# Strassen-Winograd feed-forward pairs on one Trainium2 core: the seventh product held in its place, and the first two pairs' weight sets made back to back

## The chip, the cores and the metric

The kernel runs on one core of one Trainium2 chip. The core has a matrix engine (TensorE, PE in the profile), three engines for element work (VectorE, DVE in the profile; ScalarE, ACT; GpSimd, POOL), a queue that only issues transfers (SyncE, SP), and 16 DMA engines that all queues share. PSUM is the memory that the matrix engine writes; SBUF holds everything else. The metric is the device time of one execution in microseconds (us); smaller is better.

## The reference

Two layers, each over 512 tokens of width 1024 in float32:

```python
for i in range(DEPTH):                       # 2 layers
    xn = rmsnorm(x, norm1_g[i])
    u_pool, q, k, v, g_a, g_b = split(xn @ w_in[i])
    o = diff_attention(norm_rope(q), norm_rope(k), v, lam)
    merged = sigmoid(g_a) * pool_mixer(u_pool) + sigmoid(g_b) * rmsnorm(o)
    x = x + merged @ w_out[i]
    hn = rmsnorm(x, norm2_g[i])
    gate, up = split(hn @ w_ffn_in[i])       # 1024 -> 2 x 2816
    x = x + (silu(gate) * up) @ w_ffn_out[i] # 2816 -> 1024
```

The part at hand is `hn @ w_ffn_in`, with `silu(gate) * up` behind it.

## The kernel before

Every float32 operand of the big products is cut into a high part of reduced precision (type fp32r, names ending in h or hi) and the rest (l or lo), and each product is three matmuls: high x high, high x low, low x high. The high part of a weight is a cast on ScalarE (L182), the low part a difference on VectorE (L183); `split` does both.

The feed-forward input product runs per pair of hidden blocks: a `Ffn(f0)` makes 256 gate and 256 up columns for all 512 tokens. Gate and up, and the two halves of the model width and of the tokens, are treated as a 2x2 block product in Winograd's form: seven products of 24 matmuls (128x256 each, lines L263, L265, L266 in `pair_product`) in place of eight. Each product `self.p(n, ...)` has a weight set `self.sets[n]`, a high and a low tile of 128x1024:

- 1 and 2: the weight blocks A11 and A12 themselves, made by `gate`
- 5: S1 = A21 + A22 (L654)
- 6: S2 = S1 - A11 (L656)
- 7: S3 = A11 - A21 (L655)
- 3: S4 = A12 - S2 (L663)
- 4: A22 itself

The other side of each product, sums of token blocks, is made once per layer by `Quarters.put` while the tokens' norm comes in (L360 to L369, tiles xq, xr, xt).

Two ways make a low part. `parts(src)` takes the difference on VectorE. `parts(src, piece_no)`, used for blocks that are weights as they lie in memory (A22 here), casts on ScalarE (L217), writes the negated high part to the low tile on ScalarE (L218), and lets a transfer from GpSimd's queue add the weight from HBM onto it (L219, 512 KB).

The tiles rotate: six high and six low weight tiles (`SPLITS`), seven raw tiles (`RAWS`) for loaded blocks and their sums. A set is begun when an earlier set's product has been read and its tile is free; a load is issued when a raw tile is free.

A pair's products stand in the code in the order 1, 6, 5, 2, 7, 3, 4 (`first`, `rest`, `second`): p6 and p7 go into one PSUM tile (b, an mm tile), p5 and p3 into another (c, an mm tile), p4 into a third (d, a tr tile), p1 and p2 into an sc tile. Between them ScalarE and VectorE copy and add these (L693, L696, L701, L704, L706, L711), and `swiglu` makes the hidden values (L611 to L613, fh and fl by L182 and L183).

The first two pairs of a layer, f0 = 0 and 2, are special: their sets 1 and 2 are made while the attention output is projected, p1 and p2 of both run as the tokens' norms arrive, and then `ffn_start` runs for each of the two `sums()` (the other five sets) and `rest()` (the other five products). The nine later pairs run one at a time in `ffn_in`, with `sums(True)`.

Instructions are not run in the order of the code: a scheduler that has its own costs places them on each engine, and may move an instruction ahead of others that it does not depend on. On the chip each engine then takes them strictly in that placed order.

Of the kernel before, what the change touches and what calls it, by code (L numbers as in the profile page):

```python
# [104 lines left out]
def trunk_kernel(  # L105
# [11 lines left out]
    nc = tc.nc  # L117
# [4 lines left out]
    def mm_ps():  # L122
        return ps.tile([P, 512], F32, name="mm", tag="mm", bufs=3)
# [4 lines left out]
    def tr_ps():  # L128
        return ps.tile([P, 512], F32, name="tr", tag="tr", bufs=2)
# [50 lines left out]
    def split(hi, lo, src):  # L180

        ins = nc.scalar.copy(hi, src)  # L182
        nc.vector.tensor_sub(lo, src, hi.bitcast(F32))  # L183
        return ins
# [17 lines left out]
    def loaded():  # L202

        i = at[0]
        at[0] += 1
        raw = sb.tile([P, 4, VD], F32, name="raw", tag="raw", bufs=RAWS)
        nc.sync.dma_start(raw.rearrange("p a b -> p (a b)"), wts[i])
        return i, raw

    def parts(src, piece_no=None):  # L210

        hi = sb.tile([P, 4, VD], F32R, name="whi", tag="whi", bufs=SPLITS)
        lo = sb.tile([P, 4, VD], F32R, name="wlo", tag="wlo", bufs=SPLITS)
        if piece_no is None:
            split(hi, lo, src)
        else:
            nc.scalar.copy(hi, src)  # L217
            nc.scalar.activation(lo, src, AF.Copy, scale=-1.0)  # L218
            nc.gpsimd.dma_start(lo.rearrange("p a b -> p (a b)"), wts[piece_no], accum_op=ALU.add)  # L219
        return hi, lo  # L220
# [15 lines left out]
    def run_due(done=None):  # L236

        if running[0]:
            return
        running[0] = True  # L240
        while waiting and (waiting[0][0] <= clock[0] if done is None else not done()):
            heapq.heappop(waiting)[2]()
        running[0] = False
        assert done is None or done()
# [11 lines left out]
    def pair_product(acc, a, b, start):  # L256

        for i in range(2):
            for k in range(4):
                run_due()  # L260
                ah, al = (x[:, k, i * P:(i + 1) * P] for x in a)
                bh, bl = (x[:, k, :] for x in b)
                nc.tensor.matmul(acc[:, i, :], lhsT=ah, rhs=bh, start=start and not i and not k, stop=False,  # L263
                                 skip_group_check=True)
                nc.tensor.matmul(acc[:, i, :], lhsT=ah, rhs=bl, start=False, stop=False, skip_group_check=True)  # L265
                nc.tensor.matmul(acc[:, i, :], lhsT=al, rhs=bh, start=False, stop=i == 1 and k == 3, skip_group_check=True)  # L266
                clock[0] += 3 * acc.shape[-1]

    def transpose(dst, src):
        nc.tensor.transpose(dst, src, ident)  # L270
        clock[0] += 2 * P
# [16 lines left out]
    def need(*keys):  # L288
        run_due(lambda: all(k in ready for k in keys))
# [136 lines left out]
    for layer in range(L):  # L426
# [191 lines left out]
        def hidden_pair(f0):  # L618
            tag = HIDDEN_AT[f0]
            if tag in ("u", "m", "mj"):  # L620
                hh, hl = (sb.tile([P, 2, S], F32R, name="f" + part, tag=tag, bufs=2) for part in "hl")
                return [(hh[:, i, :], hl[:, i, :]) for i in range(2)]
            tags = (("pr0", 2), ("pr1", 2)) if tag == "pr" else (("up", 2), ("us", 2))
            out = []
            for tg, bufs in tags:
                out.append([sb.tile([P, S], F32R, name="f" + part, tag=tg, bufs=bufs) for part in "hl"])
            return out

        class Ffn:
# [15 lines left out]
            def sums(self, a12=False):  # L645

                _, r21 = loaded()
                n22, r22 = loaded()
                if a12:
                    self.gate_raw(1)  # L650
                s1 = sb.tile([P, 4, VD], F32, name="ws", tag="raw", bufs=RAWS)
                if a12:
                    self.gate(0, self.n11)
                nc.vector.tensor_add(s1, r21, r22)  # L654
                nc.vector.tensor_sub(r21, self.r11, r21)  # L655
                nc.vector.tensor_sub(self.r11, s1, self.r11)  # L656
                self.sets[6] = parts(self.r11)
                self.sets[5] = parts(s1)
                if a12:
                    self.gate(1, self.n12)  # L660
                else:
                    self.sets[4] = parts(r22, n22)
                nc.vector.tensor_sub(self.r12, self.r12, self.r11)  # L663
                self.sets[7] = parts(r21)
                self.sets[3] = parts(self.r12)
                if a12:
                    self.sets[4] = parts(r22, n22)
                self.to = hidden_pair(self.f0)
                for i in range(2):
                    hidden[self.f0 + i] = self.to[i]  # L670
# [4 lines left out]
            def p(self, n, acc, start=True):  # L675
                q = quarters[-1]
                x = {1: q.b11, 2: q.b21, 3: q.b22, 4: q.t4, 5: q.t1, 6: q.t2, 7: q.t3}[n]
                pair_product(acc, self.sets[n], x, start)

            def first(self):  # L680
                self.a = s_ps().rearrange("p (i c) -> p i c", i=2)
# [7 lines left out]
            def rest(self, second=False):  # L689
                b, c = (mm_ps().rearrange("p (i c) -> p i c", i=2) for _ in range(2))  # L690
                self.p(6, b)
                x2 = self.temp("qn", 3)
                nc.vector.tensor_add(x2, b, self.x1)  # L693
                self.p(5, c)
                p5 = self.temp("ah")
                nc.scalar.copy(p5, c)  # L696
                if second:
                    self.second()
                self.p(7, b, False)
                x3 = self.temp("ta", 2)  # L700
                nc.vector.tensor_add(x3, b, self.x1)  # L701
                self.p(3, c, False)
                c22 = self.temp("pwl")
                nc.vector.tensor_add(c22, x3, p5)  # L704
                c12 = self.temp("al")
                nc.vector.tensor_add(c12, c, x2)  # L706
                swiglu(self.to, 1, c12, c22)
                d = tr_ps().rearrange("p (i c) -> p i c", i=2)
                self.p(4, d)
                c21 = self.temp("pwh")  # L710
                nc.vector.tensor_add(c21, d, x3)  # L711
                swiglu(self.to, 0, self.a, c21)

        quarters, early = [], []
# [48 lines left out]
        def ffn_start():  # L763
            need(*((f"h{layer}", t) for t in range(2)))
            for x in early:
                x.first()
            for x in early:
                x.second()
            need(*((f"h{layer}", t) for t in range(2, 4)))
            for x in early:  # L770
                x.sums()
                x.rest()

        def ffn_out(f0, f1, last):
# [78 lines left out]
```

## Time and profile before

| what | value |
|---|---|
| three runs | 1456.76, 1457.75, 1459.85 us; median 1457.75 |
| profiled execution, its own time | 1456.47 us |
| its span, first to last instruction | 1454.4 us |
| PE busy in the span | 1435.9 us (99%) |
| VectorE busy | 980.6 us (67%) |
| ScalarE busy | 692.8 us (48%) |
| mean granted TensorE clock | 0.998 |
| stretch in which the two special pairs run, layer 1 | about 379 to 432 us |
| the same in layer 2 | about 1099 to 1152 us |

The profiled execution lies 0.3 us under the fastest of the three runs; of its time 2.1 us are outside the span. Times in rows are microseconds from the span's start. In a row `mm<-xqh,wlo` names what is written and what is read. A bracket at a row's end, such as `[2.19 <-DMA wlo<-in_wts]`, is idle time of the engine just before the instruction, and what ended it. Since matmuls are pipelined, a 128x256 matmul is shown as 0.28 us long, while the next one starts 0.12 us after it. In a row of windows a pair such as `47.81 (x379)` is busy time and instructions of one engine, and the fields after POOL are the granted TensorE clock, the mean busy share of the DMA engines and GB/s.

### The profile page before, as it was taken

The page shows a single profiled execution, that of the slowest core. Times are in us where ns is not written, and L with a number is a line of the kernel's source. Part 1 is how long each engine was busy: PE and PEld are TensorE (multiplying, and loading weights), DVE is VectorE, ACT ScalarE, POOL GpSimd, SP SyncE. Part 2 cuts the span into 40 slices and gives each one's busy share as a digit, 9 for nine tenths or more (in the row PEclk, how much of TensorE's full clock was granted, in tenths as well). Part 3 has the DMA queues.
Part 4 walks back from the last instruction along what each step waited for, and adds up shares of the span by engine and source line. Part 5 has one row for each costly group of instructions (what it writes and reads, how often), then busy time and mean ns, then how long its engine had stood idle before and what let it go on. Part 6 is the DMA issues. An engine that isn't in the chain of part 4 may idle for free.

```text
span 1454.4 us, 21625 instructions
## 1 busy us (share of the span) xinstructions
PE 1435.9 (99%) x8390; PEld 1266.9 (87%) x8390; DVE 980.6 (67%) x1820; ACT 692.8 (48%) x1319; POOL 115.3 (8%) x149
## 2 busy tenths in 40 slices
PE   8999999999989999999999999999999999999999
PEld 6888888888889989989888888888888998999897
DVE  6767676666888548737576686665758985487462
ACT  6544353444656346516354443434446663464350
POOL 1010000100001001001010001001000110010000
PEclk9999999999999999999999999999999999999999
DMA  7321231224168457818422132222422683585261
GB/s 280 109 73 58 95 116 59 88 74 115 39 165 208 126 129 176 217 44 211 138 85 81 59 116 74 80 75 72 131 58 73 170 213 115 128 187 174 69 163 58
DMA packets 49208, 170.92 MB, mean 118 GB/s; under 512 B 5585, under 2 KB 6481, under 8 KB 49106
## 3 DMA queue, kind: packets, MB, share of 16 engines
q1 hardware_dynamic: 38882, 134.41, 28.2%
q0 software_dynamic: 8928, 32.51, 12.6%
q10 hardware_dynamic: 1296, 2.62, 0.6%
q8 instruction: 66, 1.08, 0.3%
q14 instruction: 36, 0.29, 0.1%
HBM read 167.42 MB, written 2.10 MB: 117 GB/s over the span
## 4 chain that ended last, share of the span: by engine, by line
PE 92%; issue 3%; DVE 2%; DMA 2%; ACT 1%; POOL 0%; POOLq 0%; DVEq 0%
PE mm L251 19%; PE mm L253 19%; PE mm L252 19%; PE mm L266 5%; PE mm L263 5%; PE mm L265 5%; PE sc L265 3%; PE sc L266 3%; PE sc L263 3%; PE tr L270 3%; DMA wlo<-in_wts 1%; PE tr L266 1%; PE tr L263 1%; PE tr L265 1%; DVE wlo L183 1%
## 5 line engine op out<-in xcount | busy, mean ns | idle before, releaser
L182 ACT CAST whi<-raw 128x1024 fp32r<-128x1024 f32 x226 | 237.4, 1052 | 210.8 <-issue 120.1
L183 DVE TENSOR_TENSOR wlo<-raw,whi 128x1024 fp32r<-128x1024 f32 x226 | 274.6, 1221 | 81.7 <-ACT whi L182 77.5
L251 PE MATMUL mm<-whi,xh 128*128 128x512 f32 x512 | 205.9, 402 | 0.2 <-ACT xh L182 0.2
L252 PE MATMUL mm<-wlo,xh 128*128 128x512 f32 x512 | 200.3, 391 | 0.4 <-DVE wlo L183 0.4
L253 PE MATMUL mm<-whi,xl 128*128 128x512 f32 x512 | 200.6, 392 | 0.0
L602 DVE TENSOR_TENSOR res<-mm,res 128x512 f32<-128x512 f32 (+1 forms) x97 | 66.1, 684 | 118.7 <-PE mm L253 118.6
L253 PE MATMUL mm<-whi,fl 128*128 128x512 f32 (+1 forms) x358 | 138.5, 387 | 0.0
L251 PE MATMUL mm<-whi,fh 128*128 128x512 f32 (+1 forms) x358 | 138.3, 387 | 0.0
L252 PE MATMUL mm<-wlo,fh 128*128 128x512 f32 (+1 forms) x358 | 138.2, 387 | 0.0
L253 PEld LDWEIGHTS mm<-whi,xl 128*128 128x128 f32 x512 | 96.2, 188 | 21.0 <-DVE xl L183 0.2
L280 POOL TENSOR_TENSOR r<-r,mhalf 128x1 f32<-128x1 f32 (+1 forms) x80 | 60.3, 754 | 673.7 <-DVE r L279 553.2
L252 PEld LDWEIGHTS mm<-wlo,xh 128*128 128x128 f32 x512 | 96.7, 189 | 18.3 <-DVE wlo L183 0.9
L251 PEld LDWEIGHTS mm<-whi,xh 128*128 128x128 f32 x512 | 96.5, 188 | 18.4 <-ACT xh L182 0.6
L266 PE MATMUL mm<-xqh,wlo 128*128 128x256 f32 x352 | 101.2, 288 | 4.7 <-DVE wlo L183 4.7
L219 POOL DMA_DIRECT2D wlo<-in_wts x62 | 54.3, 876 | 614.9 <-ACT wlo L218 328.2
L251 PE MATMUL mm<-xh,whi 128*128 128x512 f32 x256 | 102.0, 398 | 0.0
L265 PE MATMUL mm<-xql,whi 128*128 128x256 f32 x352 | 100.9, 287 | 0.0
L263 PE MATMUL mm<-xqh,whi 128*128 128x256 f32 x352 | 100.9, 287 | 0.0
L265 PE MATMUL sc<-xql,whi 128*128 128x256 f32 x352 | 99.9, 284 | 0.8 <-DVE xql L183 0.8
L253 PE MATMUL mm<-xh,wlo 128*128 128x512 f32 x256 | 99.9, 390 | 0.0
L266 PE MATMUL sc<-xqh,wlo 128*128 128x256 f32 x352 | 99.7, 283 | 0.3 <-DMA wlo<-in_wts 0.3
L263 PE MATMUL mm<-xrh,whi 128*128 128x256 f32 x352 | 99.8, 283 | 0.0
(161 smaller groups left out, 3455.0 us busy)
## 6 DMA issues: line engine op xcount, KB each, us to landing
raw<-in_wts SPq DMA_DIRECT2D x244, 512.0 KB, 4.3
wlo<-in_wts POOLq DMA_DIRECT2D x62, 512.0 KB, 7.6
pwr<-in_pool_w ACTq DMA_DIRECT2D x8, 256.0 KB, 2.7
out<-res SPq DMA_DIRECT2D x7, 256.0 KB, 2.0
res<-in_x SPq DMA_DIRECT2D x3, 512.0 KB, 8.2
g<-in_gains SPq DMA_DIRECT2D x6, 256.0 KB, 3.2
res<-in_x ACTq DMA_DIRECT2D x1, 512.0 KB, 3.9
lv<-in_rows SPq DMA_DIRECT2D x2, 256.0 KB, 5.5
```

The costliest lines, as they stand in the source:

```text
L182: ins = nc.scalar.copy(hi, src)
L183: nc.vector.tensor_sub(lo, src, hi.bitcast(F32))
L219: nc.gpsimd.dma_start(lo.rearrange("p a b -> p (a b)"), wts[piece_no], accum_op=ALU.add)
L251: nc.tensor.matmul(acc, lhsT=ah, rhs=bh, start=i == 0, stop=False)
L252: nc.tensor.matmul(acc, lhsT=ah, rhs=bl, start=False, stop=False)
L253: nc.tensor.matmul(acc, lhsT=al, rhs=bh, start=False, stop=i == n - 1)
L263: nc.tensor.matmul(acc[:, i, :], lhsT=ah, rhs=bh, start=start and not i and not k, stop=False, skip_group_check=True)
L265: nc.tensor.matmul(acc[:, i, :], lhsT=ah, rhs=bl, start=False, stop=False, skip_group_check=True)
L266: nc.tensor.matmul(acc[:, i, :], lhsT=al, rhs=bh, start=False, stop=i == 1 and k == 3, skip_group_check=True)
L270: nc.tensor.transpose(dst, src, ident)
L280: nc.gpsimd.tensor_tensor(r, r, mhalf[:, :width], op=ALU.pow)
L602: nc.vector.tensor_add(res[t][:, cs], here, res[t][:, cs])
```

## The change

Three edits. `pair_product` returns its last matmul, and `rest` places all matmuls of p4 behind the last matmul of p3 of the same pair on the matrix engine. In `sums`, for the first two pairs (a12 false), A22's set is made second, right behind set 6, and S3's set (7) comes ahead of S4's difference and set (3); the later pairs keep their order 6, 5, 2, 7, 3, 4. `ffn_start` makes the sets of both pairs before the `rest` of the first.

```diff
@@ pair_product
-                nc.tensor.matmul(acc[:, i, :], lhsT=al, rhs=bh, start=False, stop=i == 1 and k == 3, skip_group_check=True)
+                last = nc.tensor.matmul(acc[:, i, :], lhsT=al, rhs=bh, start=False, stop=i == 1 and k == 3,
+                                        skip_group_check=True)
                 clock[0] += 3 * acc.shape[-1]
+        return last
@@ Ffn.sums
                 self.sets[6] = parts(self.r11)
+                if not a12:
+                    self.sets[4] = parts(r22, n22)
                 self.sets[5] = parts(s1)
                 if a12:
                     self.gate(1, self.n12)
                 else:
-                    self.sets[4] = parts(r22, n22)
+                    self.sets[7] = parts(r21)
                 nc.vector.tensor_sub(self.r12, self.r12, self.r11)
-                self.sets[7] = parts(r21)
+                if a12:
+                    self.sets[7] = parts(r21)
                 self.sets[3] = parts(self.r12)
                 if a12:
                     self.sets[4] = parts(r22, n22)
@@ Ffn.p
-                pair_product(acc, self.sets[n], x, start)
+                return pair_product(acc, self.sets[n], x, start)
@@ Ffn.rest
-                self.p(3, c, False)
+                third = self.p(3, c, False)
...
-                self.p(4, d)
+                with tc.issue_after(third.ins):
+                    self.p(4, d)
@@ ffn_start
             for x in early:
                 x.sums()
+            for x in early:
                 x.rest()
```

No instruction and no transfer is added or taken away. On PE, outside the two special pairs of each layer (and the first matmuls of p1 of the pair behind them), the order is the same as before.

The first place is PE at the end of the first pair's p5 (tile mm_3880 before, mm_3912 in the change; tr_3995 is p4's tile, wlo_3864 the low part of A22's set, whi_3873 and wlo_3874 are set 3). Before:

```order
L265 MATMUL mm_3880<-xql_3470,whi_3859 128x256
L266 MATMUL mm_3880<-xqh_3469,wlo_3860 128x256
L263 MATMUL tr_3995<-xth_3473,whi_3863 128x256
L265 MATMUL tr_3995<-xtl_3474,whi_3863 128x256
L266 MATMUL tr_3995<-xth_3473,wlo_3864 128x256
```

With the change:

```order
L265 MATMUL mm_3912<-xql_3470,whi_3864 128x256
L266 MATMUL mm_3912<-xqh_3469,wlo_3865 128x256
L263 MATMUL mm_3912<-xqh_3469,whi_3873 128x256
L265 MATMUL mm_3912<-xql_3470,whi_3873 128x256
L266 MATMUL mm_3912<-xqh_3469,wlo_3874 128x256
```

Where p4's first matmuls stood right behind p5, p3's now stand: its first 18, then the 24 of p7, the last 6 of p3, and p4's 24.

The second place is VectorE while the last tokens' sums and the first pair's sets are made (wlo_3860 is set 5 before, wlo_3870 set 7, wlo_3874 set 3; L663 is S4, L654 the second pair's sum S1). Before:

```order
L183 TENSOR_TENSOR wlo_3860<-ws_3851,whi_3859 128x1024
L183 TENSOR_TENSOR xrl_3472<-xd_3783,xrh_3471 128x4x128
L366 TENSOR_TENSOR xd_3784<-xd_3792,tr_3772 128x512
L183 TENSOR_TENSOR xql_3470<-xd_3792,xqh_3469 128x4x128
L369 TENSOR_TENSOR xd_3785<-xw_3649,xd_3783 128x512
L183 TENSOR_TENSOR xrl_3472<-xd_3784,xrh_3471 128x4x128
L663 TENSOR_TENSOR raw_3483<-raw_3483,raw_3479 128x1024
L183 TENSOR_TENSOR xtl_3474<-xd_3785,xth_3473 128x4x128
L183 TENSOR_TENSOR wlo_3870<-raw_3847,whi_3869 128x1024
L183 TENSOR_TENSOR wlo_3874<-raw_3483,whi_3873 128x1024
L693 TENSOR_TENSOR cqn_3905<-mm_3879,cqn_3740 128x512
L654 TENSOR_TENSOR ws_4034<-raw_4030,raw_4032 128x1024
```

With the change (wlo_3869 is set 7, L667 is S4, L656 the second pair's S1, wlo_3874 set 3; set 5 stands four rows above the first one shown):

```order
L183 TENSOR_TENSOR wlo_3869<-raw_3847,whi_3868 128x1024
L183 TENSOR_TENSOR xrl_3472<-xd_3783,xrh_3471 128x4x128
L368 TENSOR_TENSOR xd_3784<-xd_3792,tr_3772 128x512
L183 TENSOR_TENSOR xql_3470<-xd_3792,xqh_3469 128x4x128
L371 TENSOR_TENSOR xd_3785<-xw_3649,xd_3783 128x512
L183 TENSOR_TENSOR xrl_3472<-xd_3784,xrh_3471 128x4x128
L667 TENSOR_TENSOR raw_3483<-raw_3483,raw_3479 128x1024
L183 TENSOR_TENSOR xtl_3474<-xd_3785,xth_3473 128x4x128
L656 TENSOR_TENSOR ws_3883<-raw_3879,raw_3881 128x1024
L183 TENSOR_TENSOR wlo_3874<-raw_3483,whi_3873 128x1024
```

Sets 5 and 7 moved up among the tokens' sums, and the second pair's S1 moved from behind set 3 to ahead of it.

The third place is VectorE at the second pair's sets (wlo_4043, wlo_4053, wlo_4057 are its sets 5, 7, 3 before). Before:

```order
L706 TENSOR_TENSOR cal_3985<-mm_3880,cqn_3905 128x512
L183 TENSOR_TENSOR wlo_4039<-raw_3481,whi_4038 128x1024
L711 TENSOR_TENSOR cpwh_4020<-tr_3995,cta_3957 128x512
L612 SCALAR_TENSOR_TENSOR th_3987<-th_3987,cal_3985 128x512
L612 SCALAR_TENSOR_TENSOR th_4022<-th_4022,sc_3685 128x512
L613 SCALAR_TENSOR_TENSOR th_3987<-th_3987,cpwl_3983 128x512
L613 SCALAR_TENSOR_TENSOR th_4022<-th_4022,cpwh_4020 128x512
L183 TENSOR_TENSOR fl_3878<-th_3987,fh_3877 128x256 x2
L183 TENSOR_TENSOR fl_3878<-th_4022,fh_3877 128x256 x2
L183 TENSOR_TENSOR wlo_4043<-ws_4034,whi_4042 128x1024
L183 TENSOR_TENSOR wlo_4053<-raw_4030,whi_4052 128x1024
L183 TENSOR_TENSOR wlo_4057<-raw_3485,whi_4056 128x1024
```

With the change (wlo_3888, wlo_3897, wlo_3901, wlo_3906 are its sets 6, 5, 7, 3):

```order
L183 TENSOR_TENSOR wlo_3888<-raw_3481,whi_3887 128x1024
L706 TENSOR_TENSOR cta_3989<-mm_3911,cqn_3740 128x512
L711 TENSOR_TENSOR cal_4017<-mm_3912,cqn_3937 128x512
L709 TENSOR_TENSOR cpwl_4015<-cta_3989,cah_3963 128x512
L183 TENSOR_TENSOR wlo_3897<-ws_3883,whi_3896 128x1024
L183 TENSOR_TENSOR wlo_3901<-raw_3879,whi_3900 128x1024
L183 TENSOR_TENSOR wlo_3906<-raw_3485,whi_3905 128x1024
L614 SCALAR_TENSOR_TENSOR th_4019<-th_4019,cal_4017 128x512
L717 TENSOR_TENSOR cpwh_4052<-tr_4027,cta_3989 128x512
```

The second pair's sets now stand ahead of the first pair's hidden values, where they stood behind them. On ScalarE the two steps of A22's set, cast and negated copy (L217, L218), likewise moved up: for the first pair the copy stands 12 instructions earlier, and for the second pair ahead of the first pair's hidden values. The order of the loads on SyncE and of the accumulating loads on GpSimd is unchanged.

## The prediction

> **What bounds the kernel now.** I read the page first, then PE's waits, the span in windows, and PE's timeline at the waits.
>
> ```profile
> span 1454.4 us, 21625 instructions
> PE 92%; issue 3%; DVE 2%; DMA 2%; ACT 1%; POOL 0%; POOLq 0%; DVEq 0%
> ```
>
> The chain that ended last is PE for 92%: the kernel goes as fast as PE is fed. So a change that leaves PE's 8390 matmuls alone can win only PE's waits, and these are few:
>
> ```profile
> PE tr L266 <- DMA wlo<-in_wts: 4.7, 2, 2.5
> PE mm L266 <- DVE wlo L183: 4.7, 2, 2.3
> PE sc L265 <- DVE xql L183: 0.8, 2, 0.4
> PE sc L266 <- DMA wlo<-in_wts: 0.3, 1, 0.3
> ...
> 379.00:432.00 53.00, 47.81 (x379) 46.87 (x379) 49.14 (x68) 32.52 (x47) 4.07 (x5) 0.97 0.45 121
> 432.00:1099.00 667.00, 666.81 (x3809) 584.98 (x3808) 440.47 (x840) 313.23 (x612) 52.73 (x66) 1.00 0.41 115
> 1099.00:1152.00 53.00, 47.72 (x381) 46.98 (x380) 48.79 (x68) 32.56 (x47) 4.06 (x5) 0.97 0.45 121
> ```
>
> Above the dots are PE's waits (total us, times, longest), below them windows. PE idles 5.2 us in 379 to 432, 5.3 us in 1099 to 1152, and 0.2 us in the 667 us between: both layers wait where the two special pairs run, and nearly nowhere else. The timeline there:
>
> ```profile
> 393.21 0.28 PE L263 MATMUL mm<-xrh,whi 128*128 128x256 f32 x1
> ...
> 398.85 0.28 PE L266 MATMUL mm<-xqh,wlo 128*128 128x256 f32 x1
> 398.97 0.28 PE L263 MATMUL tr<-xth,whi 128*128 128x256 f32 x1
> 399.09 0.28 PE L265 MATMUL tr<-xtl,whi 128*128 128x256 f32 x1
> 401.55 0.39 PE L266 MATMUL tr<-xth,wlo 128*128 128x256 f32 x1 [2.19 <-DMA wlo<-in_wts]
> ...
> 413.60 0.28 PE L265 MATMUL sc<-xql,whi 128*128 128x256 f32 x1
> 416.22 0.39 PE L266 MATMUL mm<-xqh,wlo 128*128 128x256 f32 x1 [2.34 <-DVE wlo L183]
> ```
>
> The first wait is p4 of the first pair, moved up in front of p3, with A22's low part still on its way; the second is p5 of the second pair, waiting for set 5's difference. PE steps by 0.12 us, so a matmul's tail of 0.16 us counts as busy in each wait and is lost as well. Behind the second wait the clock drops:
>
> ```profile
> 396.77:400.18 3.41, 2.60 (x22) 2.40 (x20) 3.41 (x5) 1.64 (x2) 0.00 (x0) 1.00 0.83 186
> 400.18:403.59 3.41, 2.04 (x17) 2.04 (x18) 3.34 (x4) 0.00 (x0) 0.00 (x0) 1.00 0.98 338
> 413.84:417.25 3.41, 1.07 (x9) 1.03 (x9) 3.41 (x7) 2.51 (x4) 1.44 (x2) 1.00 0.24 54
> 417.25:420.66 3.41, 3.41 (x18) 3.41 (x17) 3.38 (x5) 0.09 (x1) 0.32 (x1) 0.50 1.02 187
> 1137.46:1140.87 3.41, 3.41 (x18) 3.41 (x18) 3.38 (x5) 0.00 (x0) 0.52 (x1) 0.50 0.97 213
> ```
>
> After a stretch with 1.07 us of PE work in 3.41 the granted clock is 0.50 for the next 3.41 us, in both layers; after the first wait, spread over two such stretches (2.60 and 2.04 us of work), it stays 1.00.
>
> **What the change takes away.** First wait: 4.7 + 2 x 0.16 = 5.0 us over both layers. p4 is now behind p3 on PE, so it comes some 8 us later, and its set's copy moves up:
>
> ```profile
> 383.79 1.05 ACT L217 CAST whi<-raw 128x1024 fp32r<-128x1024 f32 x1
> 392.38 1.06 ACT L218 ACTIVATE wlo<-raw 128x1024 fp32r<-128x1024 f32 x1
> 399.17 0.59 ACT L696 COPY cah<-mm 128x512 f32<-128x512 f32 x1 [0.81 <-PE mm L266]
> 393.74 0.90 POOL L219 DMA_DIRECT2D wlo<-in_wts  x1 [9.25 <-DVE xrl L183]
> 415.76 1.81 POOL L219 DMA_DIRECT2D wlo<-in_wts  x2 [21.13 <-ACT wlo L218]
> 436.68 0.86 POOL L219 DMA_DIRECT2D wlo<-in_wts  x1 [6.13 <-ACT wlo L218]
> ...
> DMA to landing us min/median/max: 5.5/9.1/12.5
> ```
>
> L218 takes the place where L217 ran, at 383.8; the accumulating load goes out near 385.1 and, even with the longest landing here (12.5 us, 376 to 450), is in by 397.6, 9 us before p4. Second wait: 4.7 + 0.3 = 5.0 us. The second pair's set 5 now stands ahead of the first pair's hidden values on VectorE; by the rows below it is ready 2 to 3 us ahead of PE. The 0.3 us wait, with its tail 0.4, belongs to a load that went out within a microsecond of another (415.76, x2); now it goes out alone. Half clock: 2 x 3.41 x 0.50 = 3.4 us. Together 5.0 + 5.0 + 0.4 + 3.4 = 13.8 us.
>
> **What takes its place.** The first wait had hidden something: set 3 was late too.
>
> ```profile
> 395.99 1.23 DVE L663 TENSOR_TENSOR raw<-raw 128x1024 f32<-128x1024 f32 x1
> 397.13 0.69 DVE L183 TENSOR_TENSOR xtl<-xd,xth 128x512 fp32r<-128x512 f32 x1
> 397.73 2.36 DVE L183 TENSOR_TENSOR wlo<-raw,whi 128x1024 fp32r<-128x1024 f32 x2
> 400.00 0.69 DVE L693 TENSOR_TENSOR cqn<-mm,cqn 128x512 f32<-128x512 f32 x1
> 400.60 1.22 DVE L654 TENSOR_TENSOR ws<-raw 128x1024 f32<-128x1024 f32 x1
> 401.86 1.22 DVE L655 TENSOR_TENSOR raw<-raw 128x1024 f32<-128x1024 f32 x1
> ```
>
> The x2 row is sets 7 and 3: set 3 is there at 400.09. In the new order the same instructions stand ahead of it, only shuffled, and one more: the second pair's S1 (L654 before), a step of 401.86 - 400.60 = 1.26 us. So set 3 is ready at 401.35. PE starts p6 at 393.21 as before, has 48 matmuls of p6 and p5 (5.76 us) and two of p3, and asks for set 3's low part at 399.21. **New wait A: 2.2 us in each layer**, 4.4 in all. Its lower end is 0.9 us (set 3 no later than before), its upper end is the rival on the load below. From there VectorE has five steps of 1.14 to 1.26 and four of 0.6 to the start of the second pair's set 5 (third place of the change) and 1.2 for itself: 400.1 + 6.0 + 2.4 + 1.2 = 409.7. PE, at p3's third matmul at 401.35, has 94 matmuls of p3, p7, p4 and p6 (11.3 us) and two of p5, and asks at 412.9: the old second wait has 3 us of cover.
>
> p3 adds to the tile that p5 filled, so it needs p5's copy to be done: that copy began 0.32 us after p5's last matmul (398.85 to 399.17) and takes 0.59, some 1.0 us with the way back. In the first pair A covers it. In the second pair three of p3's matmuls are moved ahead of p7, behind only two of the next pair's p1, so 3 steps of 0.12 cover 0.36. **New wait B: 0.6 us a layer**, 1.2 in all; none below, since nothing else stands there, and 1.0 at most.
>
> PE then comes 6.9 - 2.2 - 0.6 = 4.1 us earlier to the next pair, whose own A22 load goes out at 436.68 and is asked for here:
>
> ```profile
> 446.62 0.28 PE L266 MATMUL tr<-xth,wlo 128*128 128x256 f32 x1
> ```
>
> With the median landing it is in at 445.8, 0.8 us ahead. If its chain of casts moves up with PE, which frees its tiles, this costs nothing; if the chain doesn't move at all, 4.1 - 0.8 = 3.3 us a layer. **New wait C: 0.5 us a layer**, nearer to nothing because every set there has a tile to wait for; 1.0 in all.
>
> The rest I cost at nothing. Set 7's cast and difference now stand ahead of the last tokens' xr parts and push these by about 1.1 us; p6's second matmul, which needs the low one, is put 14 matmuls (1.7 us) later on PE and covers it. VectorE is 49.14 of 53.0 us busy in the stretch: if it had to do all of that work within it, at most 3.9 us a layer could be won, 7.7 in all.
>
> Sum: 1456.47 - 13.8 + 4.4 + 1.2 + 1.0 = 1449.3 us on the profiled execution's scale, a gain of 7.2, just inside VectorE's 7.7. The profiled execution is 1.3 us under the median of the three runs (1457.75); half-clock stretches that fall otherwise may be why, and these go. I carry half of it: **1450.0 us**.
>
> **Rivals.** (1) The new wait A trips the half clock in both layers: 2 x 1.7 = 3.4 us more, 1453.4. For it: two waits of 2.3 us did. Against: two others as long did not, and A is shorter, with two matmuls in it. The Trainium skill ("TensorE: Matmul & The Clock Gate", section "HAM oscillation") wants PE gaps to stay under some 3.4 us; by that rule no wait here would throttle, this rival would have no chance, and 1450.0 would stand. The trace disagrees on the length and agrees that the stretch is 3.41 us, and the trace decides. (2) C at its upper end: 2 x 2.8 more, 1455.6. For it: the margin of 0.8 us; against: the chain hangs on tiles that PE frees. (3) Slower: in the new order VectorE stands at the second pair's S1 with set 3 behind it, and S1 needs the second pair's two loads. The second of these goes out when S1 of the first pair has been read for set 5, near 391.4 (set 5 starts right behind the row that began at 389.46).
>
> ```profile
> 389.46 0.69 DVE L360 TENSOR_TENSOR xd<-tr,xw 128x512 f32<-128x512 f32 x1
> ...
> DMA to landing us min/median/max: 3.2/4.8/11.1
> ```
>
> That is the landing of raw tiles (376 to 450). VectorE reaches S1 near 398.9, so the median leaves 2.7 us to spare. Each microsecond past 398.9 is one more of A. From 402.3 on, 10.9 us after issue, A is 5.6 and with the half clock the layer loses 5.6 + 1.7 + 0.6 + 0.5 = 8.4 us instead of 6.9: 1460 us with both layers and the 0.7 carried. Only the longest landing gets there, and I take that for one of the loads beside the two accumulating ones of 415.76. (4) A shrinks to 0.9 and C to nothing: 1446.4. (5) PE's order comes out of the scheduler without effect: 1457.75; the placed order shows p4 behind p3, so hardly.
>
> **How the numbers follow.** Forecast, 1446.5 to 1452.5 on its own: 0.62. Rival 1: 0.13, rival 2: 0.12, rival 3: 0.05, rival 4: 0.06, rival 5: 0.02. The range takes in rival 4 with the carried 0.7 gone, rival 1 and nearly all of rival 2: 1445.5 to 1455.0. A measurement tells 0.2%, or 2.9 us, from no change: faster means under 1454.8. That is the forecast, rival 4, most of rival 1 and under half of rival 2 (C between its ends), 0.84; rival 3 is slower, 0.05; 0.11 stay within.
>
> **What would show it.** PE's waits: "tr L266 <- DMA" and "mm L266 <- DVE" at the second pair's p5 are gone; in their stead one wait of some 2 us for VectorE's wlo at the first pair's third p3 matmul, and one of 0.6 for ScalarE's copy of p5 in the second pair. No window with clock 0.50 near 417 and 1137. VectorE's S1 of the second pair starts without waiting for a load. The 432 to 1099 stretch keeps its 0.2 us of idle time, bar C. It is wrong if p3's wait is over 4 us, if a DMA ends it, if a 0.50 window stands behind it, or if the next pair's p4 waits more than a microsecond.

## The result

| | median us | lowest to highest | runs |
|---|---|---|---|
| before | 1457.26 | 1455.62 to 1459.87 | 6 |
| changed | 1449.88 | 1448.39 to 1452.14 | 6 |

The ratio is 0.9946, 95% interval 0.9934 to 0.9959: 7.4 us or 0.5% faster. The forecast was 1450.0. A second series of the changed kernel, on the chip of the experiments, has a median of 1449.53 (0.9950, 0.9936 to 0.9963). The profiled execution took 1450.88 us.

The page and PE's waits, first of the changed kernel (total us, times, longest):

```profile
span 1449.1 us, 21617 instructions
PE 94%; DVE 4%; ACT 1%; issue 1%; POOL 0%; DMA 0%; POOLq 0%; ACTq 0%; DVEq 0%
...
PE mm L263 <- ACT cah L701: 2.6, 4, 0.8
PE mm L266 <- DVE wlo L183: 1.5, 2, 0.8
```

DMA has gone from the chain, and with it every wait of PE for an accumulating load (4.7 and 0.3 us) and for the second pair's set 5 (4.7). In their place stand waits for ScalarE's copy of p5 (cah) and for VectorE's low part of set 3. Lines behind 264 lie two or more further down than before: S1 is L656, S4 L667, x2 L698, the copy of p5 L701.

PE, VectorE and ScalarE of the changed kernel around p3 of the first pair, in layer 1:

```profile
398.59 0.28 PE L266 MATMUL mm<-xqh,wlo 128*128 128x256 f32 x1
399.70 0.38 PE L263 MATMUL mm<-xqh,whi 128*128 128x256 f32 x1 [0.83 <-ACT cah L701]
...
396.81 1.22 DVE L667 TENSOR_TENSOR raw<-raw 128x1024 f32<-128x1024 f32 x1
398.55 1.22 DVE L656 TENSOR_TENSOR ws<-raw 128x1024 f32<-128x1024 f32 x1
399.68 1.22 DVE L183 TENSOR_TENSOR wlo<-raw,whi 128x1024 fp32r<-128x1024 f32 x1
...
398.12 1.05 ACT L182 CAST whi<-raw 128x1024 fp32r<-128x1024 f32 x1 [1.17 <-DVE raw L667]
399.07 0.58 ACT L701 COPY cah<-mm 128x512 f32<-128x512 f32 x1
```

The second pair's S1 (398.55) stands ahead of set 3's low part (399.68), as the prediction said. Wait A comes in two parts: p3's first matmul waits 0.83 us for ScalarE's copy of p5, its third 0.76 us for set 3. Set 3's cast (398.12) stands ahead of that copy on ScalarE but holds it up little: the copy begins 0.48 us after p5's last matmul (398.59 to 399.07), where it was 0.32 us before.

The clock, in windows of the changed kernel (us, busy time and count of PE, PEld, DVE, ACT and POOL, then granted clock, DMA share, GB/s):

```profile
398.17:401.58 3.41, 1.82 (x13) 1.42 (x13) 3.41 (x4) 1.48 (x2) 0.00 (x0) 1.00 0.45 154
401.58:404.99 3.41, 3.41 (x18) 3.41 (x18) 3.38 (x5) 1.19 (x2) 0.00 (x0) 0.50 0.52 159
1118.38:1121.79 3.41, 3.41 (x16) 3.41 (x17) 3.38 (x4) 0.65 (x1) 0.00 (x0) 0.50 0.48 154
```

In this execution the half clock has not gone. It stands behind wait A now, in both layers. The mean clocks of the other executions show that the profiled one of the kernel before was a mild one: two 0.50 windows made 0.998 there, and of the 47 executions of that kernel beside the experiments 25 have 0.996 or less. The eleven of the changed kernel have 0.998 to 1.000. With 3.41 x 0.50 us lost to a window, 0.996 stands for about three of them (an estimate).

### The profile page after: what moved, and what is told of

Same layout as the page of the kernel before. It is cut to its first block, busy times and chain, and to the rows that moved or that the text cites. A ratio compares the mean times of both kernels' runs of the same rounds, so it can differ in the third digit from the quotient of the medians.

```text
span 1449.1 us, 21617 instructions
## 1 busy us (share of the span) xinstructions
PE 1436.7 (99%) x8390; PEld 1267.5 (87%) x8390; DVE 979.3 (68%) x1820; ACT 692.1 (48%) x1319; POOL 115.4 (8%) x149
## 4 chain that ended last, share of the span: by engine, by line
PE 94%; DVE 4%; ACT 1%; issue 1%; POOL 0%; DMA 0%; POOLq 0%; ACTq 0%; DVEq 0%
PE mm L251 20%; PE mm L253 20%; PE mm L252 20%; PE mm L266 6%; PE mm L263 6%; PE mm L265 6%; PE sc L265 3%; PE sc L266 3%; PE tr L272 3%; PE sc L263 2%; PE tr L266 1%; PE tr L263 1%; PE tr L265 1%; DVE wlo L183 1%; DVE xs L307 1%; PE sc L253 1%
## 5 line engine op out<-in xcount | busy, mean ns | idle before, releaser
L265 PE MATMUL mm<-xrl,whi 128*128 128x256 f32 x352 | 99.8, 283 | 0.0
```

## The experiments

Each ran beside the kernel before on the same chip; ratios are to that kernel, with their 95% interval.

### Which of the three edits pays

The hold of p4 is edit 1, A22's set second is edit 2, both pairs' sets made ahead is edit 3. Each of four kernels is the changed one with a part of it undone. Edit 3 undone (edits 1 and 2 left):

```diff
             for x in early:
                 x.sums()
-            for x in early:
                 x.rest()
```

Edit 1 undone (edits 2 and 3 left):

```diff
-                with tc.issue_after(third.ins):
-                    self.p(4, d)
+                self.p(4, d)
```

Edit 2 undone (edits 1 and 3 left); with edit 3 undone too, edit 1 stands alone:

```diff
-                if not a12:
-                    self.sets[4] = parts(r22, n22)
                 self.sets[5] = parts(s1)
                 if a12:
                     self.gate(1, self.n12)
                 else:
-                    self.sets[7] = parts(r21)
+                    self.sets[4] = parts(r22, n22)
                 nc.vector.tensor_sub(self.r12, self.r12, self.r11)
-                if a12:
-                    self.sets[7] = parts(r21)
+                self.sets[7] = parts(r21)
```

Edit 1 alone:

> Edit 1 alone: p4 behind p3, sets in their old order, each pair's sets before its own rest. Theory (the hold does most of it: p4's 24 matmuls now stand between the first pair's p3 and the second pair's p6 and cover set 5 of the second pair): neither of the old two waits is left, only A (about 1 us, since the second pair's S1 is not ahead of set 3) and B (0.6); 1447 to 1450. Rival (the second wait needs edit 3, as the prediction had it): PE waits 2 us or more for VectorE at the second pair's p5, 1452 to 1455.

Edits 1 and 2:

> Edits 1 and 2, without edit 3: the first pair's sets, its rest, then the second pair's sets. Theory (the second pair's S1 ahead of set 3 made wait A): A falls to 0.6 us or less, and the second pair's set 5, behind the first pair's work on VectorE again, is late by 1 to 1.5 us: about even with the changed kernel, 1448 to 1451. Rival (edit 3 is what removes the second wait of 2.5 us with its half clock): 1454 or more.

Edits 2 and 3:

> Edits 2 and 3, without edit 1: p4 is again free to stand right behind p5. Theory (p4 was in the way only because A22's set was late): with that set made second, p4 runs right behind p5 without waiting and covers A; p3 doesn't wait, and the gain shows up as waits further on, for the next pair's first sets: 1446 to 1450. Rival (p4 moved up waits for the accumulating load whatever the order of the sets): a wait of 2 us for that load is left, 1454 or more.

Edits 1 and 3:

> Edits 1 and 3 without edit 2: p4 held behind p3, both pairs' sets made ahead, but A22's set in its old place (behind set 5, set 7 after it). It closes the table of the three edits. Theory: what decides beside the hold is when ScalarE gets to the scaled copy (L218) for the third pair's A11, because its accumulating load can only leave behind it; in the two slow orders so far it left at 429.2 and 430.3 and PE stood 3.9 to 4.1 us for it. Sets made ahead push it back, A22's set in the old place too, so here that wait is back: 1455 to 1459, with p3 of the first pair waiting under 1.2 us (set 3 one step earlier than in the change). Rival: edit 2 is of no weight beside edits 1 and 3, the waits are those of the change (1.9 at p3, 0.65 at p5 of the second pair, none at the third pair): 1449 to 1451.

| edits | median us | ratio |
|---|---|---|
| 1 | 1446.90 | 0.9928 (0.9915 to 0.9940) |
| 1 and 2 | 1448.19 | 0.9937 (0.9924 to 0.9949) |
| 1 and 3 | 1460.80 | 1.0022 (1.0010 to 1.0034) |
| 2 and 3 | 1463.58 | 1.0043 (1.0030 to 1.0056) |
| 1, 2 and 3 | 1449.53 | 0.9950 (0.9936 to 0.9963) |

The hold is the whole gain: alone it is worth 10.5 us (before had 1457.43 beside it). With edit 2 it is 1.3 us slower, by overlapping intervals. Edit 3 costs 13.9 us on top of edit 1, of which edit 2 gives 11.3 back. The first two kernels came out about as their theories said; edits 2 and 3 came out as neither said (the first pair's p4 waits no more, others do), and edits 1 and 3 slower than the theory's 1459. PE's waits with edit 1 alone, and its windows, set 3's low part (the second step of the x2 row) and p3's first matmul:

```profile
PE mm L263 <- ACT cah L698: 2.3, 4, 0.7
PE sc L266 <- DMA wlo<-in_wts: 0.7, 1, 0.7
...
379.00:432.00 53.00, 50.74 (x417) 49.86 (x416) 52.53 (x72) 35.87 (x53) 4.07 (x5) 1.00 0.52 140
...
397.35 2.35 DVE L183 TENSOR_TENSOR wlo<-raw,whi 128x1024 fp32r<-128x1024 f32 x2
399.40 0.39 PE L263 MATMUL mm<-xqh,whi 128*128 128x256 f32 x1 [0.68 <-ACT cah L698]
```

Set 3 is there at 399.70 and the wait for VectorE is gone, the clock is 1.000 in all five executions, and VectorE is busy 52.53 of 53 us. The wait for p5's copy is there without set 3's cast in its way (that ended at 397.97). Counted with their tails the waits of this kernel (the two shown and one of 0.5 us) make 4.5 us against 10.4 before, so the waits give some 5.9 of the 10.5 us; the rest fits three half clocks at 1.5 us, the price read further down (an estimate).

With edits 1 and 2 the scheduler puts the first pair's p7 ahead of its p3, where it waits 0.5 us for x2, and the second pair's p5 waits for VectorE again:

```profile
PE mm L266 <- DVE wlo L183: 2.4, 2, 1.2
```

### Why some orders are slower than before

With edits 1 and 3, and with 2 and 3, PE stands for an accumulating load that is not among the change's waits: that of the third pair's A12, at its p2. (The expectations take it for A11; but p1 had ended by then, near 426.3 with edits 1 and 3, and the waiting matmuls stand behind p5, where p2 has its place.) Without the hold there are 1.4 us a layer at the second pair's p4 and 2.0 for VectorE at the third pair's p6 besides. Edits 1 and 3, then the changed kernel, each with PE's wait or use, the loads issued by SyncE and GpSimd, and VectorE around the third pair's set 5 (wlo<-ws):

```profile
437.94 0.55 PE L266 MATMUL sc<-xqh,wlo 128*128 128x256 f32 x1 [5.47 <-DMA wlo<-in_wts]
428.29 1.43 SPq L207 DMA_DIRECT2D raw<-in_wts  x2
428.42 0.86 POOL L219 DMA_DIRECT2D wlo<-in_wts  x1 [14.56 <-ACT fh L182]
wlo<-in_wts POOLq DMA_DIRECT2D x1, 512.0 KB, 9.4
...
426.40 0.69 DVE L615 SCALAR_TENSOR_TENSOR th<-th,cpwh 128x512 f32<-128x512 f32 x1
427.00 1.22 DVE L183 TENSOR_TENSOR wlo<-ws,whi 128x1024 fp32r<-128x1024 f32 x1
```

```profile
434.97 0.28 PE L266 MATMUL sc<-xqh,wlo 128*128 128x256 f32 x1
425.64 0.33 SPq L207 DMA_DIRECT2D raw<-in_wts  x1
427.71 0.86 POOL L219 DMA_DIRECT2D wlo<-in_wts  x1 [13.46 <-ACT wlo L218]
wlo<-in_wts POOLq DMA_DIRECT2D x1, 512.0 KB, 5.3
...
426.32 1.04 ACT L218 ACTIVATE wlo<-raw 128x1024 fp32r<-128x1024 f32 x1
424.40 1.21 DVE L183 TENSOR_TENSOR wlo<-ws,whi 128x1024 fp32r<-128x1024 f32 x1
```

The load leaves only 0.7 us later (428.42 against 427.71), but is under way 9.4 us instead of 5.3: two plain loads of SyncE go out within 1.5 us of it (x2 at 428.29), where the changed kernel has one, 2.1 us ahead. It is so in both layers: in the four slow orders (the two here and the two below) this load is under way 7.2 to 9.4 us, each time with one plain load within 0.5 us of it and a second within 1.4 us behind it; in the kernel before, the change and edit 1 alone it is 5.3 to 6.2 us, with the nearest plain load 1.1 to 2.1 us ahead. SyncE's first load waits for the buffer that the third pair's S1 fills until set 5's difference has read it. In the changed kernel that difference stands ahead of the second pair's hidden values (L614 from 427.14 on, then L615), in the slow order behind them.

Two more kernels met or made the same thing. The first holds the second pair's sums on VectorE behind the first pair's x2; it hands the second pair's `sums` to the first pair's `rest` as `then`:

```diff
-                nc.vector.tensor_add(x2, b, self.x1)
+                read = nc.vector.tensor_add(x2, b, self.x1)
+                if then is not None:
+                    with tc.issue_after(read.ins):
+                        then()
```

> The change with the second pair's sums held on VectorE behind the first pair's x2, so set 3 and x2 come first and the second pair's S1 after them, still ahead of the first pair's remaining output. Theory: wait A is then the copy of p5 alone (0.7 to 1.0 us), the clock stays 1.00, and the second pair's sets, some 1.8 us later than in the change, still lie ahead of its p5 (3 us of cover by the prediction): 1446.0 to 1448.0. Rival: the cover is not there, the second pair's p5 waits about as long as with the sums made pair by pair (1.45 us there): 1448.0 to 1449.5.

It took 1459.31 us (1.0012, 1.0003 to 1.0020). Both theories missed. In the two pairs the waits are as short as the first one said (0.5 us for x2 at the first pair's p7, which stands ahead of p3 here, and wait B; none for VectorE's wlo), but the third pair's load is late again:

```profile
PE sc L266 <- DMA wlo<-in_wts: 7.9, 2, 4.1
...
PE mm L263 <- DVE cqn L698: 1.0, 2, 0.5
PE mm L263 <- ACT cah L704: 1.0, 2, 0.5
```

The second holds nothing but set 5's difference of the third pair, in the changed kernel; `early[1].done` is the second pair's last L615:

```diff
+                if self.f0 == 4:
...
+                    with tc.issue_after(early[1].done.ins):
+                        nc.vector.tensor_sub(lo, s1, hi.bitcast(F32))
```

> The change with one VectorE step moved: the third pair's set 5 difference (wlo<-ws) is held behind the last product of the second pair's hidden values (L615), the place it has in the three slow orders; in the change it stands four steps ahead of them. Theory: that step frees the buffer into which SyncE loads next, so the plain load leaves some 3 to 4 us later (about 429 instead of 425.6), at the same time as the third pair's accumulating load of A11; the two and the next plain load share the transfer engines, the accumulating one is under way for 7 us or more instead of 5.3, and PE stands 3 to 5.5 us for it in each layer, with the half clock behind it: 1456 to 1462, slower than before, with the waits of the change ahead of it unmoved (1.9 at p3, 0.65 at the second pair's p5). Rival: the step's place does not matter by itself, the slow orders had other causes; the accumulating load still lands 5.3 us after it leaves and PE waits under 2 us: 1449 to 1453.

It took 1463.17 us (1.0038, 1.0024 to 1.0052). The waits ahead of it are those of the change (2.6 and 1.5 us in all), and one is new:

```profile
PE sc L266 <- DMA wlo<-in_wts: 9.6, 2, 5.9
...
432.11 0.86 POOL L219 DMA_DIRECT2D wlo<-in_wts  x1 [17.90 <-PE mm L266]
430.69 1.06 ACT L218 ACTIVATE wlo<-raw 128x1024 fp32r<-128x1024 f32 x1
```

So the place of one VectorE step, with what the scheduler moved along with it, decides between 0.5% faster and 0.4% slower. The way is only half the one that was expected. The load was under way 7.2 us in layer 1 and 9.3 in layer 2 (5.3 and 5.6 in the change), but it also left 4.4 us later (432.11 against 427.71), since ScalarE's scaled copy L218 ahead of it moved behind the hidden values' casts (from 426.32 to 430.69). How much of the loss each of the two makes differs from order to order, and no run here moves one alone.

### What makes set 3 late

The prediction laid it to the second pair's S1 on VectorE. This run gives S1 to GpSimd:

```diff
-                nc.vector.tensor_add(s1, r21, r22)
+                (nc.gpsimd if not a12 and self.f0 == 2 else nc.vector).tensor_add(s1, r21, r22)
```

> The change with one step taken off VectorE: the second pair's S1 is added by GpSimd. Theory: that one step (1.26 us) is what makes set 3 late, so the second half of wait A (0.91 us, VectorE's wlo at p3's third matmul) goes, only the first half (0.99, ScalarE's copy of p5) stays, a window loses at most 1 us and the clock stays 1.00: 1449.9 - 2 x 0.9 less the half clock of up to 2 x 1.6, so 1445.5 to 1448.0. Rival: VectorE is full anyway (51.9 of 53 us where the fill took the waits' place) and GpSimd's own step is slower than 1.22 us, so the second pair's sets come as late as before or the next wait (p5 of the second pair, or the next pair's p4) takes the 0.9 us over: 1449 to 1452.

It took 1465.68 us (1.0065, 1.0049 to 1.0082), more than either theory had. GpSimd and VectorE of that kernel, and PE's first wait:

```profile
394.67 2.39 POOL L656 TENSOR_TENSOR ws<-raw 128x1024 f32<-128x1024 f32 x1 [9.00 <-DVE xrl L183]
395.16 2.45 DVE L183 TENSOR_TENSOR xql<-xd,xqh 128x512 fp32r<-128x512 f32 x1
...
401.62 0.39 PE L263 MATMUL mm<-xqh,whi 128*128 128x256 f32 x1 [2.60 <-ACT cah L701]
```

GpSimd's step takes 2.39 us for VectorE's 1.22, and the VectorE step that begins beside it takes 2.45 us instead of 0.68 and ends 0.55 us after GpSimd is done, as if it had stood until about then (2.72 us in layer 2, with the same 0.55). The Trainium skill has this ("Trainium Architecture — The Big Picture", section "What this means for kernel authors"): the two engines share a pair of ports under an exclusive lock. The rows agree. All that follows on VectorE is 1.8 us late, set 3's cast with it, and p5's copy behind that cast; behind the pairs the third pair's loads for p1 and p2 are late as well. So the run doesn't test the theory about S1; it takes away more VectorE time than it frees.

The other runs show that S1 is only about half of it. From p5's last matmul to the end of set 3's low part it is 1.24 us in the kernel before, 1.26 with edit 1 alone, 1.82 with edits 1 and 2 and 2.31 with all three. So edit 2 makes set 3 some 0.56 us late and edit 3, with S1, 0.49. ScalarE's cast and VectorE's difference of set 3 with edits 1 and 2:

```profile
398.19 1.05 ACT L182 CAST whi<-raw 128x1024 fp32r<-128x1024 f32 x1 [1.17 <-DVE raw L667]
399.27 1.22 DVE L183 TENSOR_TENSOR wlo<-raw,whi 128x1024 fp32r<-128x1024 f32 x1
```

Edit 2 puts set 7's difference ahead of S4 on VectorE, so S4 comes later, and with it the cast that waits for S4; the difference starts only behind that cast. In the change the cast ends at 399.17, so set 3 could not have started earlier than that even without S1; it started at 399.68.

### The half clock

The first of three kernels fills wait A: 14 matmuls on data at hand, into p4's tile, which p4 overwrites, between p5 and p3 of the first pair.

```diff
+                    with tc.issue_after(fifth.ins):
...
+                        for k in range(14):
+                            fill = nc.tensor.matmul(d[:, 0, :], lhsT=ah[:, k % 4, :P], rhs=bh[:, k % 4, :], start=not k,
+                                                    stop=k == 13, skip_group_check=True)
...
+                    with tc.issue_after(fill.ins):
+                        third = self.p(3, c, False)
```

> The changed kernel with 14 matmuls more in the first pair of each layer, placed between p5 and p3, into p4's tile, which p4's first matmul overwrites; nothing else moves. Theory (half clock): in the changed kernel wait A is two waits of 0.8 us and the 0.50 clock behind them costs 1.6 us more in each layer. The 14 matmuls (1.7 us) keep PE at work through A, at most 0.4 us of waiting is left, there is no 0.50 window near 402 and 1118, and the time falls by some 3 us to about 1447. Rival (the clock is a bystander, the wait itself is the whole loss): p3 starts when it started, the time stays at 1449.9 within 1.

It took 1450.39 us (0.9952, 0.9939 to 0.9966), no gain on the change. Its clock is 1.000 in every execution and no 0.50 window stands in the pairs, so the fill did take the half clock away. But the fill (14 x 0.12 = 1.7 us a layer) stands in wait A's place and saves none of it: p3's third matmul starts at 400.84, against 400.95 in the change. And PE, earlier behind the missing half clock, now waits at the third pair's p4:

```profile
PE tr L266 <- DMA wlo<-in_wts: 1.1, 2, 0.9
```

That is wait C of the prediction, 0 in the change's first profile and 0.2 us in one layer of its second. With their tails these two waits take 1.4 us, about what one half clock costs, so no gain is left. The time, and the start of p3, came out as the rival said, though the clock is no bystander.

The change was then profiled again:

> The changed kernel once more, beside the others on the same chip. Theory: the half clock is decided in windows of 3.41 us that run freely, so where their edges fall against wait A (0.83 and 0.76 us idle, 0.6 us apart) differs from run to run; a layer whose wait falls into one window pays 1.6 us. Then the runs spread from 1448 to 1452 us with mean clocks from 1.000 to 0.998, the lower clock with the longer time, and this profile has its 0.50 windows at another place than 401.58 and 1118.38, or in one layer only, or none. Rival: the stretch trips it always: both layers every time, 1450.9 in each, and windows that start within 0.2 us of the same place behind wait A.

```profile
397.38:400.79 3.41, 1.83 (x15) 1.42 (x13) 3.41 (x5) 1.53 (x2) 0.00 (x0) 1.00 0.46 154
400.79:404.20 3.41, 3.41 (x28) 3.41 (x29) 3.38 (x4) 0.56 (x1) 0.00 (x0) 1.00 0.45 159
1114.17:1117.58 3.41, 1.83 (x13) 1.42 (x13) 3.41 (x4) 1.48 (x2) 0.00 (x0) 1.00 0.43 154
1117.58:1120.99 3.41, 3.41 (x19) 3.41 (x18) 3.38 (x5) 1.18 (x2) 0.00 (x0) 0.50 0.45 154
```

(The first two windows are laid on the grid that the second layer's 0.50 window gives.) The same program and the same waits: one layer trips, the other does not, with 1.83 us of work in 3.41 in both. The price can be read from one execution, from p3's third matmul to the first of p4:

```profile
400.79 0.39 PE L266 MATMUL mm<-xqh,wlo 128*128 128x256 f32 x1 [0.75 <-DVE wlo L183]
406.39 0.28 PE L263 MATMUL tr<-xth,whi 128*128 128x256 f32 x1
...
1116.96 0.38 PE L266 MATMUL mm<-xqh,wlo 128*128 128x256 f32 x1 [0.75 <-DVE wlo L183]
1124.08 0.28 PE L263 MATMUL tr<-xth,whi 128*128 128x256 f32 x1
```

5.60 us at full clock, 7.12 us with the half clock: 1.5 us. The change's executions follow it: mean clock 1.000 in 1448.39 and 1448.66, 0.998 in 1450.88, 1451.1 and 1452.14, 0.999 in those between.

Last, a ladder of waits behind the last output of the changed kernel: blocks of 72 to 100 matmuls of 128x256, each block's first matmul on the last result of a chain of tanh steps on ScalarE, one for each width.

```diff
+    for turn in range(5):
+        for chain in ((64,), (256,), (512,), (512, 256), (512, 512), (512, 512, 256), (512, 512, 512)):
+            acc = mm_ps()
+            n = 72 + 7 * turn
...
+                nc.scalar.activation(here[:, :w], at_[:, :w], AF.Tanh, scale=0.5)
```

> The changed kernel with a tail behind its last output: 35 blocks of 72 to 100 matmuls of 128x256, each block's first matmul waiting for a chain of ScalarE steps on the block before it, so that TensorE stands idle for seven different lengths (some 0.7 to 2.8 us), five times each. About 360 us longer, which says nothing of the change. Theory: a free window of 3.41 us with over some 1.45 us of idle time (between the 40% that did not and the 46% that did) sets the next window to 0.50. Then waits up to 1.2 us never trip it, those of 1.5 to 2.5 us do so in some of their five places and not in others, and only those near 2.8 us in nearly all. Rival: the length of the single wait decides, whatever the window: each length trips it five times or never, and lengths under 2 us never (no wait of the change alone was over 0.83 us).

The waits came out shorter than meant, 0.3 to 2.0 us. Four of its windows and what follows one of them, on the grid of its 0.50 windows, and below them one of the kernel with GpSimd's S1:

```profile
1512.73:1516.14 3.41, 1.83 (x15) 1.83 (x16) 0.00 (x0) 1.47 (x3) 0.00 (x0) 1.00 0.00 0
1587.82:1591.23 3.41, 1.40 (x12) 1.20 (x12) 0.00 (x0) 1.85 (x3) 0.00 (x0) 1.00 0.00 0
1591.23:1594.64 3.41, 3.41 (x18) 3.41 (x18) 0.00 (x0) 0.00 (x0) 0.00 (x0) 0.50 0.02 5
1659.50:1662.91 3.41, 1.61 (x14) 1.41 (x13) 0.00 (x0) 1.64 (x3) 0.00 (x0) 1.00 0.00 0
1738.00:1741.41 3.41, 2.06 (x17) 1.86 (x16) 0.00 (x0) 1.23 (x2) 0.00 (x0) 1.00 0.00 0
```

```profile
1139.85:1143.27 3.42, 1.56 (x14) 1.36 (x12) 3.42 (x9) 1.80 (x5) 0.00 (x0) 1.00 0.90 186
```

Windows with 1.40 and 1.61 us of work are followed by 0.50 (as are the only two others that tripped here, of 1.41 and 1.62), those with 1.83 and 2.06 are not. Waits of 1.79 and 2.01 us tripped it in four of their nine places, waits up to 1.35 us in none of 25. The same length does both, so the rival is out: what counts is how much of the idle time falls into one window. The bound is not quite where the theory put it (1.45 us idle, where 1.58 did not trip here). Each wait ends a matmul whose tail of 0.16 us counts as busy; without it the two tripping windows had 1.24 and 1.45 us of work, the others 1.67 and 1.90. The change's window, with two waits and so two tails, had 1.83 - 0.32 = 1.51, between the two, and there both happen. The bound isn't sharp by these rows: the last window, 1.40 us without its tail, did not trip. What else decides stays open.

### A version without the wait for p5's copy

Edit 1 alone, and p5 ahead of p6 where no second product lies between them, with its set made first:

```diff
+                if not second:
+                    self.p(5, c)
+                    nc.scalar.copy(p5, c)
                 self.p(6, b)
...
-                self.p(5, c)
```

> Edit 1 alone, and p5 with its set put ahead of p6 in every pair but the ones that go through a second product, so that p6's 24 matmuls (2.9 us) lie between p5 and p3, which waits for ScalarE's copy of p5. Theory: in the version with edit 1 alone the copy of p5 is what PE waits for (2.3 us in four waits); with cover it goes, 2 x (0.84 + 0.65) = 3.0 us less: 1443.5 to 1445.0. Rival: VectorE is what bounds the stretch there (52.5 of 53 us busy); the waits for the copy are then replaced by as long ones for VectorE's wlo of set 3 (first pair, about 0.9) and of the second pair (about 0.6): 1446.0 to 1447.5.

It took 1446.33 us (0.9927, 0.9915 to 0.9940), the same as edit 1 alone (1446.90) by their intervals. All waits for the copy are gone, and VectorE's have come in their place; the windows show why:

```profile
PE mm L266 <- DVE wlo L183: 2.3, 4, 0.8
...
379.00:432.00 53.00, 51.35 (x424) 50.53 (x423) 52.73 (x73) 36.04 (x53) 4.06 (x5) 1.00 0.53 140
```

VectorE is busy 52.73 of 53 us. That is the rival, to the row. Both versions beat the kernel before and the change (1448.39 at its lowest); what is left in this stretch is VectorE's.

## Why the prediction came out right, and where it was wrong

The time was right to 0.1 us, by errors that cancel. On the scale of the profiled execution the half clock was credited with 3.4 us, of which about 1.5 came in the median; waits A, B and C together were charged 1.5 us too much; and 0.7 us were carried.

- **What the change takes away.** Both waits and the 0.3 us one went, 10.4 us, as forecast. But the credit went to the wrong edit. The prediction gave the second wait to edit 3 (set 5 ahead on VectorE) and had edit 2 help with the first. Edit 1 alone has neither wait: p4's 24 matmuls behind p3 give both sets time enough in their old order. With edits 1 and 2, 1.2 us of the second wait come back, and edit 3 then takes them away at a price.
- **Wait A**, 2.2 us a layer: 0.99 and 0.91 us from matmul to matmul beyond the pace of 0.12, so 1.9. Its first part is p5's copy. The prediction had that copy (some 1.0 us) and said "in the first pair A covers it"; that holds for the sum, since p3's third matmul waits for set 3 in any case. What it did not see is that the copy splits A in two.
- **Set 3** was ready at 400.9 instead of 401.35, but not by the way given. "The same instructions stand ahead of it, only shuffled" left out set 3's cast on ScalarE, which the shuffle makes late: edit 2 costs 0.56 us and S1 0.49, where the prediction had 0 and 1.26.
- **Wait B**, 0.6: 0.65 in each layer.
- **Wait C**, 0.5: none. The third pair's casts moved up with PE. The mechanism is there, though: at the third pair's p4 where the fill brought PE earlier (up to 0.9 us), and at its p2, for A12 instead of A22, in the slow orders (3.0 to 5.9 us).
- **The step that failed** is rival 1, which the prediction set against the forecast: "The new wait A trips the half clock in both layers", held off because "two others as long did not, and A is shorter". By the prediction's own signs this part is wrong: a 0.50 window does stand behind A. It tripped in both layers of the profiled execution, one layer of the second, and by the clocks in no layer of the two fastest. The mistake was to weigh the length of the wait, and to take the two windows behind the old first wait (2.60 and 2.04 us of work) for proof. A is shorter, but its two halves lie so close that one window can hold both. The row that would have told was the work in a window: 3.41 less 2 us of wait is near 1.5 us, between the 1.07 that tripped and the 2.04 that did not. Neither side could be excluded there, and 0.13 was too little.
- **The sum again** with what was measured, for the profiled execution: 1456.47 - 10.4 for the waits, 3.0 for the half clocks gone and as much for those that came, + 2 x 1.9 + 2 x 0.65 = 1451.2, measured 1450.88. By the mean clocks its two half clocks are one more than the changed kernel mostly has, so 1.5 us less for the median: 1449.7, measured 1449.88. The carried 0.7 us had a true ground, half clocks that "fall otherwise": the kernel before mostly has about three, not the two of its profile. But they did not all go, and that the carried half came out right is luck.
- **VectorE's ceiling** of 7.7 us is not one. The profiled execution of edit 1 alone is 9.4 us shorter than that of the kernel before (1447.12 against 1456.47), with VectorE at 52.53 of 53 us. Part of that is the half clock; how much of the stretch's VectorE work moved behind it was not followed.
- **Rival 3**, S1 waiting for its load, did not happen: S1 began at 398.55, straight behind the step before it.

## What to carry to other kernels

Time each edit of a change by itself as well: here one of three held the whole gain, and another cost more than that until the third made up for most of it. When work is moved on an engine that is nearly full, follow what the moved steps free, buffers first, to the next loads: a step that nothing waits for directly can decide when a later load leaves, and beside which others. And judge a clock gate by the work that is left in a window wherever the window may lie, not by the longest single wait.

## What was not expected of the hardware

- The clock's windows of 3.41 us run freely against the program: the same waits of the same kernel tripped it in one layer and not in the other. The Trainium skill says so too ("TensorE: Matmul & The Clock Gate", section "What's actually happening"). The Trainium skill's section "HAM oscillation" on that page asks for gaps under some 3.4 us; here the half clock came behind two waits of 0.83 and 0.76 us close together, and behind single ones of 1.79 and 2.01 us.
- A VectorE step of two SBUF operands beside a GpSimd step took 2.45 us instead of 0.68, and 2.72 us in layer 2.
- A 512 KB accumulating load that left with two plain loads within 1.5 us was under way 9.4 us (7.2 in two other orders with the same neighbours), and 5.3 us with one plain load 2.1 us ahead of it.
